# Modulation products on VectorE alone, the mixer's gate first, branch weights loaded a part ahead

## Chip, cores and metric

The kernel runs on one core of one Trainium2 chip. The metric is the device time of one execution in microseconds (us). The time before is the median of three runs.

## What is computed

Two layers of a diffusion backbone over 256 latent tokens and 256 context tokens of width 1024. Each layer first computes six modulation vectors per stream from a conditioning vector, then four token mixers in parallel, then a mixture of experts. Cut to what the change touches:

```python
s_lat = silu(c); s_ctx = silu(c_ctx)[None]
for l in range(2):
    mod_lat = split(s_lat @ ada_w[l] + ada_b[l], 6)      # and mod_ctx likewise
    u = modulate(rms_norm(h, norm_mix_g[l]), mod[0], mod[1])
    y = token_mixer(u, ...)                              # four branches, gated, then @ w_out
    h = h + mod[2] * y                                   # the mixer's gate
    u = modulate(rms_norm(h, norm_ffn_g[l]), mod[3], mod[4])
    h = h + mod[5] * expert_choice_ffn(u)                # 16 experts
```

In layer 1 only the latent stream goes on past the keys and values.

## The kernel before, in words

**Stages.** By the profile, layer 0's mixer runs to about 710 us, its experts to about 1165, layer 1's mixer to about 1560, its experts to the end. In a mixer, TensorE (PE) multiplies the normalized tokens by the input projection. Every fp32 factor is split into a high part (a cast on ScalarE, ACT, L348) and a low part (a subtraction on VectorE, DVE, L349), and three products are summed (L355 to L357). Beside this stream run the branches: `hyena`, `conformer` (31 taps a channel on DVE, L1246), `mla` (latent attention; its softmax rows are scaled at L1418) and `diff` (differential attention). `branch` multiplies each branch's output by its weights, which it loads (L1028) and splits itself.

**Modulation.** The first two of the six vectors of layer 0 are made by PE at the start (`modulation`). All others come from `products`, as weighted sums without PE. They are made in groups `(layer, g)`, where g = 0, 1, 2 stands for vectors 0 and 1, 2 and 3, or 4 and 5. A group has 2048 outputs, in 16 chunks of 128 rows; each chunk comes in two halves of 512 weights, so a group is 32 jobs. A job loads a 128x512 weight tile (`aw`, 256 KB), multiplies it by the activated conditioning row (`cb`) and sums along the row, once for each stream that is needed: twice in layer 0, once in layer 1. Layer 0 makes the groups (0,2), (0,1) and (1,0): 96 jobs, 192 products. Layer 1 makes (1,2) and (1,1): 64 jobs, 64 products.

A product is done in one of two ways. On DVE it is one fused `scalar_tensor_tensor` that also sums (L526; the profile shows a second short instruction that reads the accumulator). On GpSimd (POOL) it is a multiplication (L528), and ACT sums it afterwards with a copy (L507). `ND` says how many of a group's 16 chunks go to DVE: 6 in layer 0, none in layer 1. So layer 0 has 72 products on DVE and 120 on POOL, layer 1 has 64 on POOL. `half(True)` issues those of DVE, `half(False)` those of POOL and ACT. `end` puts the sums together and, for g = 1 and 2, makes rows of them (L577 on POOL, then PE and ACT). The output projection waits for g = 1 (L974), `router` for g = 1 and 2.

**Order.** Instructions are issued in an order found while the kernel is built. Every part is a generator. `Order.run` goes through the list of them and takes the first that is due at the planned time of PE; a generator yields a cost per engine, an event to wait for, or the time at which it is due again. Costs are in `_a`, `_d` and `_q`: 0.60 us for a 512-wide DVE instruction, and no cost for DVE and POOL holding each other up. `PACE` is added to the planned end of a job before the next is due. `MVP` gives the place of the products in the list: 1 in layer 0, directly behind the loader of the weight stream, and 5 in layer 1. `S.wait` delays two generators by 0.7 us; it names them by their number in the whole list (41 and 51: `rope("k")` and the `end` of group (1,2) of layer 1). Each engine then works through its own queue in that order, and so does the DMA queue of SP.

**Buffers.** Twelve tiles of 128x2048 (`big`) hold the weight stream and what it multiplies; forty of 128x512 (`t2`) hold the rest. In layer 0 the conditioning rows take one `big` tile until the products are done. The residual stream `h` has eight tiles of its own; five of them hold filter tables during layer 0's mixer, and `residual` loads the tokens into all eight after `hyena` (L1618).

Of the kernel before, what the change touches and what calls it, by code (L numbers as in the profile page):

```python
# [226 lines left out]
def kernel(ctx: ExitStack, tc: tile.TileContext, x, ctxt, cols, skip, lamb, fng, ta, tb, tcn, td,  # L227
# [7 lines left out]
    NB, NT2 = 12, 40  # L235
    ND, PACE, AHEAD = (6, 0), ((0.5, -2), (3.0, -2.0)), 2
    PRE, PREW = (1, 3), (1, 3)
# [159 lines left out]
    def layer(l):  # L397
# [68 lines left out]
        def products(groups, ss, after):  # L466


            cb, cb_ev = {}, Ev()
            ends = {g: [None, None, Ev()] for g in groups}  # L470
            nd = ND[l]

            def rows():

                yield after
                if not last:
                    yield from S.until(room())
                    row = big("cb")
                for s in ss:
                    for i in range(2):  # L480
                        cb[s, i] = t2("cb") if last else row[:, (2 * s + i) * 512:(2 * s + i + 1) * 512]
                        nc.sync.dma_start(cb[s, i], bass.AP(tensor=cc.tensor, offset=cc.offset + s * D + i * 512,
                                                            ap=[[0, 128], [1, 512]]))
# [9 lines left out]
            def half(dve):  # L493
                jobs = [(lm, g, c, k) for lm, g in groups for c in (range(nd) if dve else range(nd, 16)) for k in range(2)]
                held, w = [], {}
# [7 lines left out]
                def summed(till):  # L503
                    n = 0
                    while held and held[0][2] <= till:
                        o, a, _ = held.pop(0)
                        nc.scalar.activation(o, o, AF.Copy, accum_out=a)  # L507
                        n += 1
                    return {"act": n * _a(512)}

                if jobs:
                    yield cb_ev
                    for i in range(AHEAD):
                        load(i)
                for i, (lm, g, c, k) in enumerate(jobs):
                    load(i + AHEAD)
                    wt_, arr = w.pop(i)
                    yield arr
                    if ends[lm, g][dve] is None:
                        n = nd if dve else 16 - nd  # L520
                        ends[lm, g][dve] = sm(4 * n, "ad" if dve else "ap", bufs=3).rearrange("p (s c k) -> p s c k", s=2, k=2)
                    new = []
                    for s in ss:
                        o, a = wt_ if s == ss[-1] else t2("aj" if dve else "ao"), ends[lm, g][dve][:, s, c if dve else c - nd, k:k + 1]
                        if dve:
                            nc.vector.scalar_tensor_tensor(o, wt_, 1.0, cb[s, k], op0=OP.mult, op1=OP.mult, accum_out=a)  # L526
                        else:
                            nc.gpsimd.tensor_tensor(o, wt_, cb[s, k], op=OP.mult)  # L528
                            new.append((o, a))
                    del wt_, o  # L530
                    if dve:
                        e = yield {"dve": len(ss) * (_d(512) + 0.07)}
                        yield e + PACE[l][0]
                    else:
                        e = yield {"pool": len(ss) * _q(512)}
                        yield summed(S.t["pe"])
                        held.extend((o, a, e) for o, a in new)
                        del new
                        yield e + PACE[l][1]
                    if c == (nd - 1 if dve else 15) and k == 1:  # L540
                        e = yield summed(e)
                        ends[lm, g].append(e)
                        if len(ends[lm, g]) == 3 + (0 < nd) + (nd < 16):
                            ends[lm, g][2].t = max(ends[lm, g][3:]) + 1.0
                            if not last and (lm, g) == groups[-1]:
                                drop()

            def end(lm, g, r):
                m = mods[lm]
                yield ends[lm, g][2]  # L550
                dst = m["B" if g == 0 else f"c{g}"]
                n = r.stop - r.start
                for dve, c0, c1 in ((True, 0, nd), (False, nd, 16)):
                    if c1 > c0:
                        a, t = ends[lm, g][dve], sm(32, "as", bufs=1).rearrange("p (s c) -> p s c", s=2)[:, r, c0:c1]
                        nc.vector.tensor_tensor(t, a[:, r, :, 0], a[:, r, :, 1], op=OP.add)
                        nc.vector.scalar_tensor_tensor(dst[:, r, c0:c1], t, 0.5, col(lm, "ada_b")[:, None, g * 16 + c0:g * 16 + c1]
                                                       .to_broadcast([128, n, c1 - c0]), op0=OP.mult, op1=OP.add)
                if g != 1:
# [26 lines left out]

            return [end(lm, g, slice(ss[0], 2)) for lm, g in groups] + [rows(), half(True), half(False)]

# [271 lines left out]
        h_ev = {(t, n): Ev() for t in tchunks for n in range(4)}  # L860
        gates_done, br_ev = Ev(), Ev()

        def stream(items):
# [65 lines left out]
            def body():  # L929
# [43 lines left out]
                gates_done.t = S.t["pe"]  # L973
                yield mods[l]["ev"][1]  # L974
                for k in range(KC):
                    yield acc_ev[k]
# [37 lines left out]

        def branch(i, os, k0, ready):
            nk = len(os)
            yield ready
            if not accs:
                yield from S.until(room(ns))
                accs.extend(big("acc") for _ in range(ns))  # L1020
            ws, arr = {}, {}
# [19 lines left out]

            CUT = {"act": nk / 2 * _a(512), "dve": nk / 2 * _d(512)}
            for d2 in range(BA[l]):
                load(d2)
            yield tg_ev[i, 0]
            yield arr[0]
# [264 lines left out]
        kv_n, cq_n = {}, {}  # L1311
        ml_done = Ev()
        o_ml = [None] * 2
# [20 lines left out]
        def mla():  # L1334
# [69 lines left out]
            del wuq, wukv, cqT, kvT, krT  # L1404
            yield e
            scale = 96.0 ** -0.5
            for c in range(2):
# [206 lines left out]
        def residual():  # L1614
            yield hy_done
            for t in range(4):
                for n in range(2):
                    nc.sync.dma_start(h[t][n], tokens(t)[:, n * 512:(n + 1) * 512])  # L1618

        head, body = stream(items)  # L1620
# [8 lines left out]
        if l == 0:  # L1629
            gens += [lambdas(), residual()]  # L1630
        gens += [hyena(), mla(), rope("k"), rope("q"), diff(),
                 branch(1, o_hy, 4, hy_done), branch(2, o_cf, 6, cf_done), branch(3, o_ml, 8, ml_done),
                 branch(0, o_df, 0, df_done)]
        mv = products([(l, 2), (l, 1)] + ([] if last else [(l + 1, 0)]), (1,) if last else (0, 1), u_ev)
        mv_at = MVP[l]
# [9 lines left out]
        xe, top = {}, {}  # L1645
        rt_ev, x_ev = Ev(), [Ev(), Ev()]
        r_tok = [const.tile([128, 1], F32, name=f"rtok{l}{t}") for t in range(4)]
# [78 lines left out]
        def router():  # L1726
# [14 lines left out]
            nc.vector.tensor_copy(cb[:, :R], p[:, :R])  # L1741
            yield {"pe": 1.0, "dve": 0.1}

        def route(t):

            s, i = t // 2, streams.index(t // 2)
            s4, ss = sm(4, "ss4"), sm(1, "ss")
            b, e, hT = t % 2, 0.0, None

            def logits(n):  # L1750
# [402 lines left out]
```

## Time and profile before

| | |
|---|---|
| median of 3 runs | 2030.7 us (2025.22 to 2036.47) |
| the profiled execution | 2030.58 us, of which the span from first to last instruction is 2028.8 us |
| busy, share of the span | PE 84%, DVE 48%, ACT 28%, POOL 25% |
| mean granted clock of TensorE | 0.907 |
| moved by DMA | 550.75 MB, 271 GB/s over the span |

The shares are means over stages with different limits. The stages are told apart by the windows, which give the busy time of each engine in a stretch of the span.

### The profile page before, as it was taken

The page shows a single profiled execution, that of the slowest core. Times are in us where ns is not written, and L with a number is a line of the kernel's source. Part 1 is how long each engine was busy: PE and PEld are TensorE (multiplying, and loading weights), DVE is VectorE, ACT ScalarE, POOL GpSimd, SP SyncE. Part 2 cuts the span into 40 slices and gives each one's busy share as a digit, 9 for nine tenths or more (in the row PEclk, how much of TensorE's full clock was granted, in tenths as well). Part 3 has the DMA queues.
Part 4 walks back from the last instruction along what each step waited for, and adds up shares of the span by engine and source line. Part 5 has one row for each costly group of instructions (what it writes and reads, how often), then busy time and mean ns, then how long its engine had stood idle before and what let it go on. Part 6 is the DMA issues. An engine that isn't in the chain of part 4 may idle for free.

```text
span 2028.8 us, 28213 instructions
## 1 busy us (share of the span) xinstructions
PE 1713.3 (84%) x11128; PEld 1109.7 (55%) x11128; DVE 973.3 (48%) x1690; ACT 573.0 (28%) x1301; POOL 503.6 (25%) x413
## 2 busy tenths in 40 slices
PE   5889787899999899989999789988998867676665
PEld 2669465676788844334333268877997433322222
DVE  4787898977644412223332176778665111111012
ACT  4443454544432110001100063566552000000000
POOL 1565797803110100000010033777321000000000
PEclk8998888999999999989999999998998977777677
DMA  7534534331235599999999964555579999999997
GB/s 277 192 110 133 177 125 139 114 113 52 67 98 220 181 343 399 418 416 417 415 415 419 410 198 144 161 181 176 169 234 355 405 411 413 415 414 411 414 414 295
DMA packets 204589, 550.75 MB, mean 271 GB/s; under 512 B 14054, under 2 KB 94120, under 8 KB 173992
## 3 DMA queue, kind: packets, MB, share of 16 engines
q1 hardware_dynamic: 204456, 548.94, 71.7%
q8 instruction: 88, 1.44, 0.3%
q14 instruction: 45, 0.37, 0.0%
HBM read 547.83 MB, written 1.05 MB: 271 GB/s over the span
## 4 chain that ended last, share of the span: by engine, by line
PE 46%; DMA 28%; DVE 15%; ACT 4%; issue 3%; POOL 3%; SPq 0%; ACTq 0%; DVEq 0%; POOLq 0%
PE pm L1973 10%; DMA we<-in_w_eo_dram 10%; DMA we<-in_w_ei_dram 9%; PE pm L355 6%; PE pm L357 6%; PE pm L356 6%; PE psc L1998 4%; DMA h<-in_w_ei_dram 3%; DMA h<-in_w_eo_dram 3%; DVE wq L349 3%; PE psc L1862 2%; DVE aj L526 1%; DVE aw L526 1%; ACT wq L348 1%; POOL aw L528 1%
## 5 line engine op out<-in xcount | busy, mean ns | idle before, releaser
L1973 PE MATMUL pm<-we,xe 128*32 128x256 f32 (+1 forms) x2912 | 407.1, 543 | 97.9 <-DMA we<-in_w_ei_dram 96.0
L1973 PEld LDWEIGHTS pm<-we,xe 128*32 128x32 f32 (+1 forms) x2912 | 136.0, 136 | 345.2 <-issue 186.9
L355 PE MATMUL pm<-uh,wq 128*128 128x256 f32 (+1 forms) x832 | 293.6, 353 | 17.7 <-ACT tg L1001 8.2
L356 PE MATMUL pm<-ul,wq 128*128 128x256 f32 (+1 forms) x832 | 285.7, 343 | 2.5 <-DVE ul L785 1.5
L357 PE MATMUL pm<-uh,wq 128*128 128x256 f32 (+1 forms) x832 | 285.0, 342 | 0.0
L349 DVE TENSOR_TENSOR wq<-wi,wq 128x1024 fp32r<-128x1024 f32 x131 | 182.5, 1404 | 114.0 <-ACT wq L348 113.9
L1985 DVE SCALAR_TENSOR_TENSOR ea<-ea,pm 128x512 f32<-128x512 f32 (+1 forms) x32 | 17.7, 554 | 428.5 <-ACT ea L1984 428.5
L1998 PE MATMUL psc<-we,eaT 128*32 128x256 f32 (+1 forms) x1280 | 171.6, 510 | 35.0 <-DMA we<-in_w_eo_dram 33.5
L528 POOL TENSOR_TENSOR aw<-aw,cb 128x512 f32<-128x512 f32 x124 | 192.8, 1568 | 16.7 <-DMA aw<-in_ada_t_dram 8.1
L355 PEld LDWEIGHTS pm<-uh,wq 128*128 128x128 f32 x832 | 163.4, 196 | 41.4 <-ACT tg L1001 9.1
L356 PEld LDWEIGHTS pm<-ul,wq 128*128 128x128 f32 x832 | 163.1, 196 | 20.6 <-issue 3.7
L357 PEld LDWEIGHTS pm<-uh,wq 128*128 128x128 f32 x832 | 163.4, 196 | 16.8
L2010 DVE TENSOR_TENSOR ye<-psc,modr 32x512 f32<-32x512 f32 (+1 forms) x120 | 66.4, 554 | 201.8 <-PE psc L1998 200.5
L1984 ACT ACTIVATE ea<-pm 128x512 f32<-128x512 f32 (+1 forms) x32 | 15.7, 491 | 483.1 <-PE pm L1973 483.1
L348 ACT CAST wq<-wi 128x1024 fp32r<-128x1024 f32 x132 | 136.2, 1044 | 15.2 <-DMA wi<-in_w_in_dram 13.0
L1998 PEld LDWEIGHTS psc<-we,eaT 128*32 128x32 f32 (+1 forms) x1280 | 58.7, 129 | 143.8 <-issue 74.3
L1902 POOL TENSOR_TENSOR hg<-h,gr 128x512 f32<-128x512 f32 x2 | 2.6, 1286 | 462.0 <-DMA gr<-in_fng_dram 458.1
L1246 DVE SCALAR_TENSOR_TENSOR ca<-up,colt,ca 128x510 f32<-128x510 f32 (+29 forms) x120 | 113.4, 945 | 2.3
L528 POOL TENSOR_TENSOR ao<-aw,cb 128x512 f32<-128x512 f32 x60 | 97.7, 1628 | 22.5 <-DMA aw<-in_ada_t_dram 19.5
L2042 ACT COPY eaT<-pt 128x512 f32<-128x512 f32 (+1 forms) x32 | 15.3, 479 | 273.9 <-PE pt L2040 273.9
L1292 ACT ACTIVATE e<-psc,nm 128x512 f32<-128x512 f32 (+1 forms) x72 | 44.3, 616 | 146.5 <-DVE nm L1290 146.1
L660 POOL MEMSET hf<- 1x256 f32 x4 | 1.5, 378 | 325.8 <-ACT ab L656 325.8
(408 smaller groups left out, 3005.0 us busy)
## 6 DMA issues: line engine op xcount, KB each, us to landing
we<-in_w_ei_dram SPq DMA_DIRECT2D x233, 1024.0 KB, 14.0
we<-in_w_eo_dram SPq DMA_DIRECT2D x110, 1024.0 KB, 14.6
wi<-in_w_in_dram SPq DMA_DIRECT2D x58, 1024.0 KB, 5.4
aw<-in_ada_t_dram SPq DMA_DIRECT2D x160, 256.0 KB, 5.5
we<-in_w_ei_dram SPq DMA_DIRECT2D x52, 256.0 KB, 8.1
wbr<-in_w_branch_dram SPq DMA_DIRECT2D x40, 256.0 KB, 5.3
h<-in_w_ei_dram SPq DMA_DIRECT2D x40, 256.0 KB, 16.3
h<-in_w_eo_dram SPq DMA_DIRECT2D x40, 256.0 KB, 16.3
```

What stands on the lines that cost most here:

```text
L348: nc.scalar.copy(hi, src)
L349: eng.tensor_tensor(lo, src, hi.bitcast(F32), op=OP.subtract)
L355: nc.tensor.matmul(out, lh, rh, start=first and i == 0, stop=False)
L356: nc.tensor.matmul(out, lh, rl, start=False, stop=False)
L357: nc.tensor.matmul(out, ll, rh, start=False, stop=last and i == n - 1)
L526: nc.vector.scalar_tensor_tensor(o, wt_, 1.0, cb[s, k], op0=OP.mult, op1=OP.mult, accum_out=a)
L528: nc.gpsimd.tensor_tensor(o, wt_, cb[s, k], op=OP.mult)
L1246: nc.vector.scalar_tensor_tensor(o, up[:, :, max(d, 0):256 + min(d, 0)], cw[:, c0 + d:c0 + d + 1], o, op0=OP.mult, op1=OP.add)
L1292: nc.scalar.activation(e, p[:, :nk], AF.Exp, scale=scale, bias=nm, accum_out=s)
L1973: nc.tensor.matmul(dst[j * M:(j + 1) * M, :], lhs, w[o + j * FW // 512][:, j * FW % 512:j * FW % 512 + FW], start=k == 0, stop=k == KC - 1 ...
L1998: nc.tensor.matmul(py[j * M:(j + 1) * M, :FW], aT[:, c * 128 + q * M:c * 128 + (q + 1) * M], w[f % 2 * 2 + j * FW // 512][:, j * FW % 512: ...
L2010: nc.vector.tensor_tensor(ye[eg][s][c0 // 512][e4 * CAP:(e4 + 1) * CAP, c0 % 512:c0 % 512 + FW], py[r0:r0 + CAP, :FW], mod5[r0:r0 + CAP, c ...
```

## The change

All products are fused instructions on DVE; `half` is one generator. The order of groups is (l,1), (l,2), then (1,0) in layer 0. The pace is 0.0 in layer 0 and -1.5 in layer 1. In layer 1 the rows are loaded and the products begin once the latent tokens are normalized (`lat_ev`), before the context's are. In layer 0 the conditioning rows lie in three tiles of `h` and one `t2` tile; so `residual` loads five tiles after `hyena` and three after the last product, and the output projection waits for that in the plan. `branch` loads its first weights at an earlier event (`early`) than that of its input. `route` waits for `router` in the plan. With one generator less per layer, numbers 41 and 51 of the list are `rows` and `conformer` of layer 1.

```diff
-    ND, PACE, AHEAD = (6, 0), ((0.5, -2), (3.0, -2.0)), 2
+    PACE, AHEAD = (0.0, -1.5), 2
...
             def rows():
                 yield after
-                if not last:
-                    yield from S.until(room())
-                    row = big("cb")
                 for s in ss:
                     for i in range(2):
-                        cb[s, i] = t2("cb") if last else row[:, (2 * s + i) * 512:(2 * s + i + 1) * 512]
+                        cb[s, i] = t2("cb") if last or (s, i) == (0, 0) else h[s + 2][i]
...
-                        o, a = wt_ if s == ss[-1] else t2("aj" if dve else "ao"), ends[lm, g][dve][:, s, c if dve else c - nd, k:k + 1]
-                        if dve:
-                            nc.vector.scalar_tensor_tensor(o, wt_, 1.0, cb[s, k], op0=OP.mult, op1=OP.mult, accum_out=a)
-                        else:
-                            nc.gpsimd.tensor_tensor(o, wt_, cb[s, k], op=OP.mult)
-                            new.append((o, a))
+                        o = wt_ if s == ss[-1] else t2("aj")
+                        nc.vector.scalar_tensor_tensor(o, wt_, 1.0, cb[s, k], op0=OP.mult, op1=OP.mult,
+                                                       accum_out=ends[lm, g][0][:, s, c, k:k + 1])
                     del wt_, o
-                    if dve:
-                        e = yield {"dve": len(ss) * (_d(512) + 0.07)}
-                        yield e + PACE[l][0]
-                    else:
-                        e = yield {"pool": len(ss) * _q(512)}
-                        yield summed(S.t["pe"])
-                        held.extend((o, a, e) for o, a in new)
-                        del new
-                        yield e + PACE[l][1]
+                    e = yield {"dve": len(ss) * (_d(512) + 0.07)}
+                    yield e + PACE[l]
+                    if c == 15 and k == 1:
+                        ends[lm, g][1].t = e + 1.0
+                prod_ev.t = e
...
                 yield mods[l]["ev"][1]
+                if l == 0:
+                    yield res_ev
...
-        def branch(i, os, k0, ready):
+        def branch(i, os, k0, ready, early):
             nk = len(os)
-            yield ready
-            if not accs:
-                yield from S.until(room(ns))
-                accs.extend(big("acc") for _ in range(ns))
...
+            yield early
             for d2 in range(BA[l]):
                 load(d2)
+            yield ready
+            if not accs:
+                yield from S.until(room(ns))
+                accs.extend(big("acc") for _ in range(ns))
...
         def residual():
-            yield hy_done
-            for t in range(4):
-                for n in range(2):
+            for ev, part in ((hy_done, range(5)), (prod_ev, range(5, 8))):
+                yield ev
+                for i in part:
+                    t, n = i // 2, i % 2
                     nc.sync.dma_start(h[t][n], tokens(t)[:, n * 512:(n + 1) * 512])
+                yield S.load(0.25 * len(part))
+            res_ev.t = 0.0
...
-                 branch(1, o_hy, 4, hy_done), branch(2, o_cf, 6, cf_done), branch(3, o_ml, 8, ml_done),
-                 branch(0, o_df, 0, df_done)]
-        mv = products([(l, 2), (l, 1)] + ([] if last else [(l + 1, 0)]), (1,) if last else (0, 1), u_ev)
+                 branch(1, o_hy, 4, hy_done, k_ev), branch(2, o_cf, 6, cf_done, cfa_ev[1][0]),
+                 branch(3, o_ml, 8, ml_done, ml_mid), branch(0, o_df, 0, df_done, df_mid)]
+        mv = products([(l, 1), (l, 2)] + ([] if last else [(l + 1, 0)]), (1,) if last else (0, 1), lat_ev if last else u_ev)
...
-            yield {"pe": 1.0, "dve": 0.1}
+            rw_ev.t = yield {"pe": 1.0, "dve": 0.1}
         def route(t):
...
+            yield rw_ev
```

## Rows read from the trace of the kernel before

**Rows 1.** The page: busy us (share) x instructions; busy tenths in 40 slices of 50.7 us

```profile
PE 1713.3 (84%) x11128; PEld 1109.7 (55%) x11128; DVE 973.3 (48%) x1690; ACT 573.0 (28%) x1301; POOL 503.6 (25%) x413
...
DVE  4787898977644412223332176778665111111012
...
DMA  7534534331235599999999964555579999999997
```

**Rows 2.** Windows: length, busy of PE, PEld, DVE, ACT, POOL, then PEclk, DMA share, GB/s

```profile
50.00:400.00 350.00, 288.93 (x1310) 221.60 (x1311) 301.00 (x416) 165.07 (x406) 254.03 (x183) 0.90 0.43 142
400.00:620.00 220.00, 214.11 (x1114) 171.26 (x1114) 137.29 (x267) 95.37 (x199) 35.26 (x32) 1.00 0.27 82
...
720.00:1165.00 445.00, 416.21 (x1914) 157.29 (x1912) 113.01 (x201) 36.70 (x71) 6.93 (x9) 0.97 1.01 406
...
1200.00:1450.00 250.00, 222.34 (x1641) 200.10 (x1640) 194.82 (x306) 142.87 (x342) 154.96 (x125) 0.96 0.52 165
...
1560.00:2029.00 469.00, 319.23 (x3341) 138.04 (x3340) 72.20 (x178) 22.35 (x58) 3.68 (x4) 0.76 0.99 399
```

**Rows 3.** Waits of PE, 40 to 400 us: total us, times, longest

```profile
PE pt L1298 <- DVE e L1418: 16.1, 4, 8.1
PE psc L1369 <- DVE rp L1360: 9.6, 1, 9.6
...
PE psc L357 <- DVE wbrl L349: 4.5, 2, 2.9
```

**Rows 4.** The chain that ended last, 0 to 720 us: start, us, what

```profile
203.93 4.39 DVE wq L349 x2
208.32 1.69 DVE aj L526 x2
...
213.60 1.98 PE psc L1369 x2
```

**Rows 5.** Lines 526 and 528, 0 to 420 us: ns min/median/max, first and last start

```profile
L526 DVE SCALAR_TENSOR_TENSOR aj<-aw,cb x36: 624/1632/1809, 86.1 to 391.3; 128x512 f32<-128x512 f32 x36
...
L526 DVE DVE_READ_ACCUMULATOR aj<-aw,cb x36: 73/77/84, 87.8 to 393.0; 128x1 f32 x36
L526 DVE SCALAR_TENSOR_TENSOR aw<-aw,cb x36: 691/1631/1819, 87.9 to 393.1; 128x512 f32<-128x512 f32 x36
...
L528 POOL TENSOR_TENSOR ao<-aw,cb x60: 1255/1712/2291, 89.0 to 399.0; 128x512 f32<-128x512 f32 x60
```

**Rows 6.** Windows of lines 526 (DVE), 528 (POOL, both stretches) and 507 (ACT, both) alone

```profile
50.00:400.00 350.00, 95.92 (x144) 0.90 0.43 142
...
50.00:400.00 350.00, 191.56 (x119) 0.90 0.43 142
1200.00:1450.00 250.00, 95.61 (x64) 0.96 0.52 165
...
50.00:400.00 350.00, 77.27 (x235) 0.90 0.43 142
1200.00:1450.00 250.00, 42.84 (x128) 0.96 0.52 165
```

**Rows 7.** Lines of DVE, 50 to 400 us: busy us, mean ns; idle before, releaser

```profile
L1246 DVE SCALAR_TENSOR_TENSOR ca<-up,colt,ca 128x510 f32<-128x510 f32 (+14 forms) x43 | 52.5, 1221 | 0.8
L349 DVE TENSOR_TENSOR wq<-wi,wq 128x1024 fp32r<-128x1024 f32 x33 | 52.3, 1596 | 22.4 <-ACT wq L348 22.4
```

**Rows 8.** The same view, 420 to 700 us, where no products run

```profile
L349 DVE TENSOR_TENSOR wq<-wi,wq 128x1024 fp32r<-128x1024 f32 x30 | 37.7, 1263 | 47.1 <-ACT wq L348 47.1
...
L1246 DVE SCALAR_TENSOR_TENSOR ca<-up,colt,ca 128x490 f32<-128x490 f32 (+4 forms) x10 | 7.2, 722 | 0.2
```

**Rows 9.** Waits of PE, 1165 to 1560 us

```profile
PE pm L355 <- ACT tg L1001: 8.2, 4, 6.2
```

**Rows 10.** The chain that ended last, 1130 to 1560 us

```profile
1383.50 6.96 POOL aw L528 x5
```

**Rows 11.** Tile wbr, its DMA issues on SP: ns min/median/max, first and last start

```profile
L1028 SPq DMA_DIRECT2D wbr<-in_w_branch_dram x40: 368/379/1633, 201.0 to 1513.5; - x40
```

More of the change, by code (lines that the diff above doesn't have):

```diff
@@ L469, in products @@
             cb, cb_ev = {}, Ev()
-            ends = {g: [None, None, Ev()] for g in groups}
-            nd = ND[l]
+            ends = {g: [None, Ev()] for g in groups}
             def rows():
                 yield after
-                if not last:
-                    yield from S.until(room())
-                    row = big("cb")
                 for s in ss:
                     for i in range(2):
-                        cb[s, i] = t2("cb") if last else row[:, (2 * s + i) * 512:(2 * s + i + 1) * 512]
+                        cb[s, i] = t2("cb") if last or (s, i) == (0, 0) else h[s + 2][i]
                         nc.sync.dma_start(cb[s, i], bass.AP(tensor=cc.tensor, offset=cc.offset + s * D + i * 512,
@@ L491, in rows, with half @@
                 cb_ev.t = S.t["dve"]
-            def half(dve):
-                jobs = [(lm, g, c, k) for lm, g in groups for c in (range(nd) if dve else range(nd, 16)) for k in range(2)]
-                held, w = [], {}
+            def half():
+                jobs = [(lm, g, c, k) for lm, g in groups for c in range(16) for k in range(2)]
+                w = {}
                 def load(i):
@@ L501, in load @@
                         w[i] = load2(ada_t[lm, r:r + 128, k * 512:(k + 1) * 512], "aw"), S.load(0.25)
[L503 to L514, printed above, removed]
+                yield cb_ev
+                for i in range(AHEAD):
+                    load(i)
                 for i, (lm, g, c, k) in enumerate(jobs):
@@ L518, in half @@
                     yield arr
[L519 to L522, printed above, removed]
+                    if ends[lm, g][0] is None:
+                        ends[lm, g][0] = sm(64, "ad", bufs=3).rearrange("p (s c k) -> p s c k", s=2, k=2)
                     for s in ss:
-                        o, a = wt_ if s == ss[-1] else t2("aj" if dve else "ao"), ends[lm, g][dve][:, s, c if dve else c - nd, k:k + 1]
-                        if dve:
-                            nc.vector.scalar_tensor_tensor(o, wt_, 1.0, cb[s, k], op0=OP.mult, op1=OP.mult, accum_out=a)
-                        else:
-                            nc.gpsimd.tensor_tensor(o, wt_, cb[s, k], op=OP.mult)
-                            new.append((o, a))
@@ L530, in half @@
-                    del wt_, o
-                    if dve:
-                        e = yield {"dve": len(ss) * (_d(512) + 0.07)}
-                        yield e + PACE[l][0]
-                    else:
-                        e = yield {"pool": len(ss) * _q(512)}
-                        yield summed(S.t["pe"])
-                        held.extend((o, a, e) for o, a in new)
-                        del new
-                        yield e + PACE[l][1]
[L540 to L546, printed above, removed]
+                        o = wt_ if s == ss[-1] else t2("aj")
@@ L549, in end @@
                 m = mods[lm]
-                yield ends[lm, g][2]
+                yield ends[lm, g][1]
                 dst = m["B" if g == 0 else f"c{g}"]
                 n = r.stop - r.start
[L553 to L558, printed above, removed]
+                a, t = ends[lm, g][0], sm(32, "as", bufs=1).rearrange("p (s c) -> p s c", s=2)[:, r]
@@ L559, in end @@
+                nc.vector.tensor_tensor(t, a[:, r, :, 0], a[:, r, :, 1], op=OP.add)
+                nc.vector.scalar_tensor_tensor(dst[:, r], t, 0.5, col(lm, "ada_b")[:, None, g * 16:g * 16 + 16]
+                                               .to_broadcast([128, n, 16]), op0=OP.mult, op1=OP.add)
                 if g != 1:
@@ L585, in end @@
                 m["ev"][g].t = e
-            return [end(lm, g, slice(ss[0], 2)) for lm, g in groups] + [rows(), half(True), half(False)]
+            return [end(lm, g, slice(ss[0], 2)) for lm, g in groups] + [rows(), half()]
         def filters(lf, after=None):
@@ L860, in layer @@
         h_ev = {(t, n): Ev() for t in tchunks for n in range(4)}
-        gates_done, br_ev = Ev(), Ev()
+        gates_done, br_ev, prod_ev, res_ev = Ev(), Ev(), Ev(), Ev()
         def stream(items):
@@ L1311, in layer @@
         kv_n, cq_n = {}, {}
-        ml_done = Ev()
+        ml_done, ml_mid = Ev(), Ev()
         o_ml = [None] * 2
@@ L1405, in mla @@
             yield e
+            ml_mid.t = e
             scale = 96.0 ** -0.5
@@ L1645, in layer @@
         xe, top = {}, {}
-        rt_ev, x_ev = Ev(), [Ev(), Ev()]
+        rt_ev, rw_ev, x_ev = Ev(), Ev(), [Ev(), Ev()]
         r_tok = [const.tile([128, 1], F32, name=f"rtok{l}{t}") for t in range(4)]
```

## The prediction

> **What bounds the kernel now.** I read the page first: its engine line and slices [rows 1]. No engine is the bound everywhere. DMA reads 9 tenths only in two stretches, and DVE is high only in two others. The windows by stage [rows 2] put numbers on that. The experts of layer 0 (720 to 1165) and of layer 1 (1560 to 2029) run at a DMA share of 1.01 and 0.99: they last as long as their weights take to arrive, and the change leaves their bytes alone. They only start earlier or later, with the end of the mixer before them. The products, as the kernel calls the weighted sums, lie in two stretches: 50 to 400 us in layer 0 and 1200 to 1450 in layer 1. The forecast is made there.
>
> In 50 to 400 PE is busy 288.9 of 350 us, so it stands idle for 61 us, and its mean granted clock is 0.90. The clock knows 2.4 and 1.2 GHz; 10% below full over 350 us is worth 35 us. From 400 to 620 PE is busy 214 of 220 at clock 1.00: there nothing is to be had [rows 2]. So in layer 0 at most some 61 us of idle time and a part of the 35 us can come back.
>
> Who makes PE wait in 50 to 400? The list of waits names DVE: 16.1 us for the scaled attention rows of L1418, 9.6 us for one rope step [rows 3]. The chain of that place shows how such a wait is made: two weight splits take 4.39 us and a product 1.69 us, both ahead of the rope step for which PE waits until 213.6 [rows 4]. Both are stretched. A fused product takes 0.62 to 0.69 us at its shortest and 1.63 at the median; a POOL product takes 1.26 at its shortest and 1.71 at the median [rows 5]. The same split takes 1.60 us in this stretch and 1.26 in 420 to 700, where no products run; a convolution tap takes 1.22 against 0.72 [rows 7, 8]. So DVE and POOL hold each other up, and a third of the products on DVE already costs 95.9 us [rows 6].
>
> **Part 1, layer 0: 120 products go from POOL to DVE.** POOL loses 191.6 of its 254.0 us and ACT loses 77.3 of accumulation [rows 2, 6]. DVE work, at quiet prices:
> - products: 192 x (0.69 + 0.08 us for reading the accumulator) = 148 [rows 5], in place of 96 for 72;
> - all else: 301.0 - 95.9 = 205; less 43 taps x 0.50 = 21.5 and 33 splits x 0.33 = 11 [rows 7, 8], so 172.6.
>
> That makes 320 us against 301 now. DVE gets no lighter: what 120 products add (92) is somewhat more than what the contention gives back (46 on its own products, 32 on taps and splits). To it comes the contention with the other 62.5 us of POOL work: nothing at least; at most every us of it, 62.5. The rows show 78 us lost for 254 us of POOL work, 0.31 each, so 19; some of that is still within the 172.6, since I took the stretch off taps and splits alone. I take 10, near that row: 330.
>
> Trainium skill, "SBUF — State Buffer", Who interferes with whom: the shared port pair is an exclusive lock, held for a whole instruction, and a DVE instruction with two SBUF inputs contends with a POOL instruction that reads SBUF. By that rule alone a pair would take 0.69 + 1.26 = 1.95 us and all 62.5 us of the other POOL work would count, so that the sum of DVE would be 382. The trace agrees on who contends, but its pairs go by in about 1.7. By the lock alone the stretch would be 382 + 15 - 25 = 372 us, 22 more than now, on the side of the slower rival below.
>
> DVE's idle time is 49 us now, 22.4 of it waits for ACT's half of a split [rows 2, 7]. ACT gets 77 us back and a product fills any gap, so I leave 15 (from 0 to 49). Not all products need lie in this stretch: DVE has 220 - 137 = 83 us idle from 400 to 620 [rows 2]. The last of the three groups, 64 products or 49 us, serves layer 1 alone. The planner gives a product its turn when DVE's planned queue has run down (place 1 in the list, pace 0), so only some slip over; I take 25 us (from 0 to 49). Length of the stretch: 330 + 15 - 25 = 320, **30 us less**. Ends: 320 + 0 - 49 = 271, but PE's own work is 289 - 35 = 254 and never ran gapless, so 290, 60 less; above, 330 + 49 - 0 = 379, 29 more.
>
> Why should PE go along? Its waits are for DVE results behind a queue, and each block in that queue gets shorter: a pair of products 1.54 us instead of 3.3, a split 1.26 instead of 1.60. And the planner costs a pair at 1.35 us: the order written by it is near to what the chip does when nothing stretches.
>
> **Part 2, layer 1: 64 products, all on POOL now, go to DVE.** POOL loses 95.6 us of 155, ACT 42.8 [rows 2, 6]. Here the products stand in the way on those two: PE waits 8.2 us for ACT's gate tanh [rows 9], and 7 us of the chain are POOL products in a row [rows 10], with the normalization of the differential heads behind them in POOL's order. DVE is busy 194.8 of 250; with 49 more that is 244 if contention gives nothing back, or 205 if it gives back the fifth that it takes from DVE's other work in layer 0 (32.5 of 205, and some on smaller operations). The products may start once the latent rows are normalized, so before 1200, which spreads them further. PE's idle time is 27.7 us and its clock 0.96 is worth 10 [rows 2]. I take **10 us less**; ends 25 less (most of the idle time) and 15 more (a third of the 49 us on the path).
>
> **The small parts.** Branch weights a part ahead: no wait on their DMA is in the list; the 4.5 us of PE are for their split on DVE [rows 3], counted above. The 40 issues of 0.38 us [rows 11] on SP only move; ahead of a wi load they cost it that much and the ring's weights lie ready. I take 0, up to 5 more if the held buffers delay others. Residual loads in two parts: 3 of 8 issues move behind the products, hidden by the 220 us of gates and branches before the output projection; if the plan's end of the products is too early, SP stands in that wait with the wi loads behind it: 0 to 10 more. The freed `big` buffer, the mixer's gate first, and the router's wait: 0, since PE has only 6 us of idle time in 400 to 620, where the modulation would be waited for. The planner's two 0.7 us delays now fall on other workers (the rows and the conformer of layer 1): 0, either sign, a few us.
>
> **Sum.** The profiled execution took 2030.58 us, as the median of 2030.7. 2030.6 - 30 - 10 = **1990 us**. Added ends: 2030.6 - 60 - 25 = 1945 and 2030.6 + 29 + 15 + 5 + 10 = 2090.
>
> **Rivals.**
> - *VectorE becomes the bound (slower).* Place: 50 to 400, where DVE wants 330 us at least if all products come early, as place 1 in the list makes them. If DVE keeps its present share of the stretch, 301 of 350 (0.86), it needs 330 / 0.86 = 384, 34 more; with layer 1 level, **2065**. It decides from the point where DVE is busy over 95% of the stretch and PE's waits on it pass the 61 us of idle. For it: 0.86 already, and 120 products more on the fullest engine. Against: the gaps in DVE's row are waits that products can fill. Trainium skill, "Perfetto Trace Analysis", Optimizing Scalar/DVE Operations: when DVE is saturated, moving work to ScalarE or GpSimd may make sense, though between DVE and GpSimd it might not help. The first half speaks against this change, the second for its being a wash; the trace has both, 0.86 busy and pairs at 1.7. Chance 0.2.
> - *A wash.* Shorter blocks, but 2.7 times as many, and PE waits as long as before: 350 + 0 to 10 less in layer 0, 0 in layer 1: **2025**. Speaks for it that DVE's sum hardly changes. Chance 0.18.
> - *Nearly all waits go.* PE runs the stretch as it runs 400 to 620: 60 less, and 25 less in layer 1: **1945**. Against it: DVE must shed 49 us past 400. Chance 0.1.
> - *It doesn't do what it says*: SP stuck behind the late residual loads, or the branch loads crowding out others. It would be seen as DMA waits before splits; 10 us, within the wash.
>
> **How the numbers follow.** Forecast 0.52 (1965 to 2015 by itself), all waits 0.1, wash 0.18, slower 0.2. A measurement of this kernel tells about 0.5%, 10 us, from no change. Faster than 2020.5: 0.52 + 0.1 + 0.03 of the wash = 0.65. Within: 0.16, the rest of the wash and a little of the slower case. Slower than 2041: 0.19. The range goes from 1955 to 2048: it leaves out half of the case below and some 0.14 above.
>
> **What would show it.** Right: products at about 0.7 us and splits at 1.25 throughout; DVE over 90% busy up to some 370 us; PE idle under 40 us in 50 to 400 with the clock above 0.93; no POOL product and no accumulation on ACT; the experts' stages as long as before, only earlier. Wrong: DVE at 97% with PE idle above 60 us (the slower rival), products still at 1.2 us or more (the remaining POOL work costs what the lock says), or a gain that is lost again between 400 and 720.

## The result and the profile after

The changed kernel takes 2001.56 us (median of 4 runs, 1998.93 to 2005.31) against 2029.6 for the kernel before in the same comparison: a ratio of 0.9874, 95% interval 0.9853 to 0.9894, 28 us less. The forecast was 1990, 40 less.

The page of the changed kernel: busy times, and slices of 50.0 us.

```profile
PE 1700.4 (85%) x11128; PEld 1108.5 (55%) x11128; DVE 971.6 (49%) x2052; ACT 461.8 (23%) x933; POOL 217.3 (11%) x229
...
PE   5998999887999899899899788998988867666665
...
DVE  4886789877764312212432285888864111111012
...
PEclk8999999888999899989999998999998877787777
DMA  7443334423345799999999954565759999999997
```

Against [rows 1], POOL lost 286 us and ACT 111, and DVE's total stayed where it was: the products that came added about as much busy time as the shorter instructions gave back. The windows by stage, with the columns of [rows 2]:

```profile
50.00:370.00 320.00, 305.08 (x1585) 244.81 (x1582) 259.32 (x540) 112.52 (x213) 58.89 (x56) 0.98 0.41 134
370.00:600.00 230.00, 190.84 (x856) 148.36 (x855) 172.91 (x380) 75.94 (x154) 39.08 (x38) 0.90 0.34 108
...
696.00:1140.00 444.00, 416.45 (x1916) 157.63 (x1914) 112.95 (x201) 36.70 (x71) 6.92 (x9) 0.97 1.01 408
1175.00:1425.00 250.00, 232.98 (x1725) 212.18 (x1725) 198.76 (x429) 110.67 (x225) 63.11 (x64) 0.96 0.56 179
...
1535.00:2002.00 467.00, 316.81 (x3340) 137.94 (x3340) 67.04 (x160) 22.36 (x58) 3.66 (x4) 0.77 0.99 397
```

Layer 0 is told by two windows. From 50 to 370 us PE has done 1585 matmuls; before, it had done 1310 from 50 to 400. It idles 15 us of 320, with the clock at 0.98. Then it turns: from 370 to 600 PE stands idle for 39 us with the clock at 0.90, where the kernel before, from 400 to 620, had 6 us at 1.00. By 600 it has done 2441; before, 2424 by 620. The kernel before reaches 1585 matmuls at 441 us:

```profile
50.00:441.00 391.00, 329.93 (x1585) 255.99 (x1586) 332.68 (x484) 186.34 (x457) 256.12 (x184) 0.91 0.41 137
```

So, counted in matmuls done, a lead of 71 us at 370 has shrunk to some 20 at 600. The experts' stages keep their length (444 and 467 us) and DMA share, and only start earlier.

The instructions themselves became what the forecast said. The products' own line, one half of those of layer 0 (ns min/median/max, first and last start):

```profile
L510 DVE SCALAR_TENSOR_TENSOR aw<-aw,h x96: 691/692/1660, 82.3 to 583.7; 128x512 f32<-128x512 f32 x96
L510 DVE DVE_READ_ACCUMULATOR aw<-aw,h x96: 76/81/85, 83.8 to 584.3; 128x1 f32 x96
```

The median fell from 1.63 us [rows 5] to 0.69. But the last product starts at 584 us, not at 399. The windows of this line alone show how the products spread:

```profile
50.00:370.00 320.00, 84.55 (x224) 0.98 0.41 134
370.00:600.00 230.00, 63.60 (x160) 0.90 0.34 108
```

What PE waits for from 370 to 600 (total us, times, longest):

```profile
PE psc L355 <- ACT wbrh L348: 21.9, 3, 12.4
PE psc L355 <- ACT e L1264: 5.7, 3, 3.3
PE pt L1230 <- DVE ol L1510: 4.0, 1, 4.0
```

In the kernel before, all of PE's waits listed for 40 to 400 add up to 49.0 us that end with DVE, 11.3 with ACT and 5.8 with POOL. In the changed kernel, 40 to 370, they are 12.8 with DVE, 7.1 with ACT and none with POOL. Of the two longest of [rows 3] the first is gone, and of the other this is left:

```profile
PE psc L1341 <- DVE rp L1332: 2.3, 1, 2.3
```

Behind 370, PE waits mostly for casts of branch weights on ACT, and ACT in that stretch waits for DVE:

```profile
ACT e L1264 <- DVE nm L1262: 53.4, 18, 6.6
```

### The profile page after: what moved, and what is told of

Read it like the earlier page. It is cut to its first block, busy times and chain, and to the rows that moved or that the text cites. A ratio compares the mean times of both kernels' runs of the same rounds, so it can differ in the third digit from the quotient of the medians.

```text
span 2001.9 us, 27922 instructions
## 1 busy us (share of the span) xinstructions
PE 1700.4 (85%) x11128; PEld 1108.5 (55%) x11128; DVE 971.6 (49%) x2052; ACT 461.8 (23%) x933; POOL 217.3 (11%) x229
## 4 chain that ended last, share of the span: by engine, by line
PE 48%; DMA 26%; DVE 14%; issue 6%; ACT 5%; POOL 1%; SPq 0%; ACTq 0%; DVEq 0%; POOLq 0%
DMA we<-in_w_ei_dram 14%; PE pm L1951 10%; DMA we<-in_w_eo_dram 7%; PE pm L355 7%; PE pm L357 6%; PE pm L356 6%; PE psc L1976 4%; DVE wq L349 3%; DMA h<-in_w_eo_dram 3%; PE psc L1840 2%; DVE aw L510 2%; PE psc L355 2%; ACT wq L348 1%; PE psc L357 1%; PE psc L356 1%
## 5 line engine op out<-in xcount | busy, mean ns | idle before, releaser
L349 DVE TENSOR_TENSOR wq<-wi,wq 128x1024 fp32r<-128x1024 f32 x131 | 164.1, 1263 | 91.9 <-ACT wq L348 91.5
L1218 DVE SCALAR_TENSOR_TENSOR ca<-up,colt,ca 128x510 f32<-128x510 f32 (+29 forms) x120 | 80.8, 673 | 2.1
L355 PE MATMUL pm<-wq,uh 128*128 128x256 f32 (+1 forms) x240 | 72.7, 303 | 8.1 <-DVE rsq L319 4.0
L510 DVE SCALAR_TENSOR_TENSOR aw<-aw,h 128x512 f32<-128x512 f32 x96 | 77.1, 803 | 3.6
L356 PE MATMUL pm<-wq,uh 128*128 128x256 f32 (+1 forms) x240 | 70.7, 295 | 0.0
L357 PE MATMUL pm<-wq,ul 128*128 128x256 f32 (+1 forms) x240 | 70.7, 295 | 0.0
```

The source lines that it names most:

```text
L349: eng.tensor_tensor(lo, src, hi.bitcast(F32), op=OP.subtract)
L355: nc.tensor.matmul(out, lh, rh, start=first and i == 0, stop=False)
L356: nc.tensor.matmul(out, lh, rl, start=False, stop=False)
L357: nc.tensor.matmul(out, ll, rh, start=False, stop=last and i == n - 1)
L1218: nc.vector.scalar_tensor_tensor(o, up[:, :, max(d, 0):256 + min(d, 0)], cw[:, c0 + d:c0 + d + 1], o, op0=OP.mult, op1=OP.add)
```

## The experiments

All times are medians in us, with the ratio to the kernel before of the same comparison. Where stages are compared, this table holds; its marks are read from one profiled execution of each kernel, so a few us between two rows mean little: the first gated product of the output projection in layer 0, the first matmul with the output weights of layer 0's last expert, the first gated product in layer 1, and the time from the second to the third.

```
run                        layer 0   last expert   layer 1   length
before                       646.3        1164.5    1531.9    367.4
changed                      622.4        1139.4    1502.1    362.7
products alone               638.5        1154.6    1511.5    356.9
branch loads late            625.5        1142.9    1516.6    373.7
POOL reads back              693.4        1211.2    1623.1    411.9
short products               590.7        1107.4    1454.7    347.3
short POOL products          580.0        1097.2    1436.7    339.5
pace early                   616.6        1133.5    1497.2    363.7
rows in big                  622.9        1139.8    1504.7    364.9
order back                   609.1        1127.1    1492.7    365.6
branch loads early alone     644.2        1162.5    1532.9    370.4
order back, loads late       622.5        1138.4    1512.6    374.2
order back, pace early       624.4        1140.9    1508.5    367.6
order back, measured costs   635.4        1154.0    1518.5    364.5
```

**1. Products alone**, in the kernel before:

```diff
-    ND, PACE, AHEAD = (6, 0), ((0.5, -2), (3.0, -2.0)), 2
+    ND, PACE, AHEAD = (16, 16), ((0.0, -2), (-1.5, -2.0)), 2
```

> The kernel before with nothing changed but where the products run: all 16 chunks on DVE in both layers, pace 0.0 and -1.5. Branch loads, order of groups, buffers and residual loads stay as before. If the gain comes from taking the products off POOL and ACT: 2000 to 2010 us, a ratio to before of 0.985 to 0.990, products at 0.7 us and splits at 1.25 us. If it comes from the other parts of the change (branch weights ahead, the freed buffer, the order of groups): 2020 to 2035 us.

Measured: 2017.88 (2011.89 to 2018.73), ratio 0.9952 (0.9932 to 0.9973). Between the two: some four tenths of the gain. The profiled run is the fastest of its runs, 6 us under the median, so its row in the table flatters it. There layer 1 gains 10.5 us, as the forecast had it, and layer 0 only 8.

**2. Branch loads late**, in the changed kernel:

```diff
-branch(1, o_hy, 4, hy_done, k_ev), branch(2, o_cf, 6, cf_done, cfa_ev[1][0])
-branch(3, o_ml, 8, ml_done, ml_mid), branch(0, o_df, 0, df_done, df_mid)
+branch(1, o_hy, 4, hy_done, hy_done), branch(2, o_cf, 6, cf_done, cf_done)
+branch(3, o_ml, 8, ml_done, ml_done), branch(0, o_df, 0, df_done, df_done)
```

> The changed kernel with the branch weights loaded when the branch's input is ready, as before. If that part is worth nothing, as forecast: within 5 us of the changed kernel, 1997 to 2007 us. If it carries a part of the gain: 2010 us or more, with PE waiting for casts of branch weights that stand behind a DMA.

Measured: 2019.47 (2015.16 to 2026.29), ratio 0.9966 (0.995 to 0.9983), 0.9% or 18 us above the changed kernel. A part that I had put at nothing carries more than the products do alone. The table puts 3 us of it into layer 0 and 11 into layer 1. SP's queue of this run at that place (start, us, what, how many) and the chain there show the 11:

```profile
1487.13 9.79 SPq L1678 DMA_DIRECT2D we<-in_w_ei_dram  x5
1497.02 1.88 SPq L1676 DMA_DIRECT2D we<-in_w_ei_dram  x4
1498.99 0.44 SPq L995 DMA_DIRECT2D wbr<-in_w_branch_dram  x1
```

```profile
1497.94 0.12 PE psc L355
1498.99 10.32 DMA wbr<-in_w_branch_dram
1509.39 0.63 ACT wbrh L348
1510.06 0.58 PE psc L355
```

The last part of the branch weights, 256 KB, is issued behind nine loads of expert weights, 6 MB together, that SP has just sent off. It lands 10.3 us later, where the median of these loads in this run is 5.1. ACT, DVE and PE all stand. Loaded a part ahead, it goes out before the experts'.

**3. POOL reads back**, in the changed kernel:

```diff
-                        o = wt_ if s == ss[-1] else t2("aj")
+                        o = t2("aj")
+                        for q in range(3 if last or c >= 6 else 0):
+                            nc.gpsimd.tensor_tensor(scr, wt_[:, q * 160:q * 160 + 192], cb[s, k][:, q * 160:q * 160 + 192], op=OP.mult)
```

> The changed kernel with three POOL multiplications of 192 columns of the same weight tile added beside as many products as POOL had before (120 and 64); their result goes to a scratch tile that nobody reads, the plan doesn't count them, the output stays the same. If contention between POOL and DVE is the mechanism: products and splits get back to 1.2 us and more, and the time goes to 2035 us or above, beyond the kernel before, since DVE now carries all products. If the engine that does the products matters only through POOL's and ACT's queues or through the order: 2000 to 2015 us.

Measured: 2124.09 (one run), 122 above the changed kernel, in both mixers (71 us by the output projection of layer 0, 49 in the length of layer 1). DVE's lines in 50 to 400 (busy us, mean ns):

```profile
L513 DVE SCALAR_TENSOR_TENSOR aj<-aw,h 128x512 f32<-128x512 f32 x84 | 78.3, 956 | 0.5 <-POOL scr L512 0.5
L349 DVE TENSOR_TENSOR wq<-wi,wq 128x1024 fp32r<-128x1024 f32 x39 | 53.5, 1383 | 21.8 <-ACT wq L348 21.8
```

DVE's instructions stretch (means of 0.96 and 1.38 against 0.74 and 1.22 in the changed kernel up to 370), less than I expected, and the time goes further up than I expected. What this run can't tell apart: the added work also stands in POOL's queue in front of work for which the mixers wait, and the products' results take a tile more.

**4. Short products**, in the changed kernel:

```diff
-nc.vector.scalar_tensor_tensor(o, wt_, 1.0, cb[s, k], ...
+nc.vector.scalar_tensor_tensor(o[:, :32], wt_[:, :32], 1.0, cb[s, k][:, :32], ...
```

> The changed kernel with each product over 32 of 512 columns, so that the sums leave out the rest; the order, the loads and the waits stay. DVE loses some 130 us of work in layer 0 and 30 in layer 1. If the products still hold PE up (PE idle between 370 and 600 us, where DVE is shared by products, attention rows and branch splits): 1965 to 1985 us. If DVE no longer matters: 1995 to 2003 us.

Measured: 1956.34 (1952.94 to 1959.94), ratio 0.9662 (0.9639 to 0.9685): 43 us below the changed kernel by the ratios, more than expected, though DVE's products lost only 95 us in layer 0 (148 to 53), not 130. The products' time on DVE is still on the path. PE's window and its longest wait (the window 370 to 580 here, 370 to 600 for the wait):

```profile
370.00:580.00 210.00, 189.68 (x887) 150.05 (x888) 133.55 (x367) 77.60 (x154) 34.91 (x38) 0.95 0.37 122
```

```profile
PE psc L355 <- ACT wbrh L348: 18.3, 3, 10.3
```

PE idles 20 us there, against 39 in the changed kernel. But its waits for casts of branch weights hardly shrink (18.3 against 21.9 us), so most of them do not come from the length of the products. The same waits are 20.4 us in run 1 and about 1 in the kernel before and in run 5: they are there where the plan puts all products on DVE.

**5. Short POOL products**, in the kernel before:

```diff
-nc.gpsimd.tensor_tensor(o, wt_, cb[s, k], op=OP.mult)
+nc.gpsimd.tensor_tensor(o[:, :32], wt_[:, :32], cb[s, k][:, :32], op=OP.mult)
...
-nc.scalar.activation(o, o, AF.Copy, accum_out=a)
+nc.scalar.activation(o[:, :32], o[:, :32], AF.Copy, accum_out=a)
```

> The kernel before with each POOL product and its sum on ACT over 32 of 512 columns, so that those sums leave out the rest; order, loads and waits stay, and 72 products stay on DVE at full width. It shows what POOL's products and ACT's sums cost before the change, without more work on DVE. If contention and those two queues hold the mixers up: splits at 1.25 us, 1955 to 1980 us in all. If DVE's own work is the bound and POOL's part was hidden: 2010 to 2028 us.

Measured: 1933.16 (1930.98 to 1936.11), ratio 0.9539 (0.9499 to 0.958), 92 us less. So POOL's products and their sums at full width cost 92 us while they ran beside everything else. The lines of DVE in 50 to 400 and the windows:

```profile
L349 DVE TENSOR_TENSOR wq<-wi,wq 128x1024 fp32r<-128x1024 f32 x41 | 50.6, 1245 | 52.3 <-ACT wq L348 52.3
...
L526 DVE SCALAR_TENSOR_TENSOR aw<-aw,cb 128x512 f32<-128x512 f32 x36 | 27.3, 757 | 1.2
```

```profile
50.00:370.00 320.00, 302.69 (x1568) 240.02 (x1567) 241.08 (x478) 140.08 (x455) 120.22 (x185) 0.97 0.48 163
370.00:580.00 210.00, 203.91 (x995) 162.81 (x995) 122.75 (x227) 83.25 (x162) 33.17 (x30) 1.00 0.30 100
```

With POOL's reads cut short the split takes 1.25 and the product 0.76, and PE goes as fast to 370 as in the changed kernel. PE's waits in 40 to 400 that end with DVE fall from 49.0 to 10.8 us, those with ACT stay (11.3 and 11.6), those with POOL fall from 5.8 to 0.9: what comes back reaches PE through DVE. How much of the 92 us is the stretch of DVE's instructions and how much the queues of POOL and ACT further back, no run separates. In the 210 us from 370 to 580 DVE has only 123 us of work, against 159 in the changed kernel:

```profile
370.00:580.00 210.00, 170.84 (x766) 131.81 (x765) 158.75 (x353) 68.66 (x142) 38.46 (x37) 0.89 0.35 111
```

PE idles 6 us there, against 39. This is the gain of the change without its price, since 120 products are cut short here and none is moved.

**6. Pace early**, in the changed kernel: `PACE` of layer 0 from 0.0 to -1.5.

> The changed kernel with the pace of layer 0's products at -1.5 in place of 0.0, so that they are planned earlier and closer together. If the products' late end (584 us, in the stretch of the differential attention) is what eats a part of the gain: they end before 500 us and the output projection starts earlier than at 622 us, 1985 to 1997 us. If VectorE becomes the bound as soon as products crowd in front of hyena and mla: the output projection starts later and the time is 2008 to 2025 us.

Measured: 1996.75 (1995.5 to 2000.11), ratio 0.986 (0.9819 to 0.99). The products end at 495 us and the output projection starts 6 us earlier; the intervals of the two ratios overlap. It is not slower, so crowding the products is no harm by itself; that their late end was the price is not shown: 43 us of products are left after 370 in place of 64, and PE still idles 32 us between 370 and 600.

**7. Rows in big**, in the changed kernel: the conditioning rows of layer 0 in a `big` tile (as in the lines taken out above), `drop()` after the last group, and

```diff
-            for ev, part in ((hy_done, range(5)), (prod_ev, range(5, 8))):
+            for ev, part in ((hy_done, range(8)),):
```

> The changed kernel with layer 0's conditioning rows in one of the twelve big tiles again, and all residual loads after hyena, as before. Products alone brought the output projection of layer 0 8 us forward, the whole change 24; late branch loads cost 3 of it. If the freed big tile is the rest: the output projection of layer 0 starts at 632 to 640 us and the time is 2010 to 2018 us. If it is not (order of groups, numbers in the list): within 4 us of the changed kernel.

Measured: 2002.91 (1998.13 to 2006.41), ratio 0.9878 (0.9836 to 0.9919). The freed tile is worth nothing that these times show.

**8. Order back**, in the changed kernel: `products([(l, 2), (l, 1)] + ...`.

> The changed kernel with the groups in the order (l,2), (l,1) again. Nothing waits for the gate before the output projection, which comes after the last product: if so, within 4 us of the changed kernel, 1997 to 2006 us. If the order is what the rest of the gain in layer 0 hangs on: 2010 us or more.

Measured: 1990.14 (1989.67 to 1992.96), ratio 0.9822 (0.9782 to 0.9861): a miss on the good side. It ran on the same chip as run 7, whose fastest run is above its slowest. So "the mixer's gate first" costs some 11 us by the ratios, whose intervals just overlap (13 against run 7); in the profiled executions all of it lies in layer 0. PE's windows are the same up to 370; the difference lies behind it:

```profile
50.00:370.00 320.00, 305.01 (x1588) 244.83 (x1587) 259.77 (x541) 112.80 (x214) 61.17 (x64) 0.98 0.40 134
370.00:600.00 230.00, 201.14 (x912) 156.65 (x911) 179.43 (x386) 78.98 (x158) 37.40 (x30) 0.93 0.35 117
```

912 matmuls in place of 856, and 11.6 us of waits for casts of branch weights in place of 21.9. Of all kernels that compute everything, this one was the fastest.

**9. Branch loads early alone**, in the kernel before: the new `branch` with its four events, and nothing else.

> The kernel before with nothing changed but the branch weights, loaded at the earlier events; the products stay on POOL and DVE. In the trace of before no cast of branch weights waited for a DMA. If early loads pay only once the mixer runs faster (as the late ones cost 18 us in the changed kernel): within 6 us of before, 2019 to 2031 us. If they are worth 18 us by themselves: 2003 to 2012 us.

Measured: 2037.5 (2027.88 to 2042.86), ratio 1.0045 (1.0021 to 1.007). A miss: no gain by itself but a loss of some 9 us, with the interval clear of 1. Where it is lost no run shows; by the table it is in neither mixer to more than 3 us.

**10. Order back, loads late**, in the changed kernel: runs 2 and 8 together.

> The changed kernel with both undone: groups in the order (l,2), (l,1) and branch weights loaded late. With early loads the old order gave 1990 us. If the two parts add up: 2004 to 2012 us. If they are tied to each other, by the plan that comes out of both: 1990 to 2000 or 2015 to 2025 us. Products alone gave 2018 us; where this is near, the freed buffer, the earlier start in layer 1 and the numbers in the list are worth nothing.

Measured: 2017.03 (2012.29 to 2018.47), ratio 0.9934 (0.991 to 0.9959). By the ratios the old order gives 0.3% with late loads (against run 2) and 0.5% with early ones (run 8 against the changed kernel), and the intervals overlap in both. If the parts simply added up, the ratio would be 0.991, which is just inside the interval. That they are tied is so only in the profiled executions, where the old order brings the output projection of layer 0 forward by 3 us with late loads and by 13 with early ones; the times do not show it. This kernel is also where the products alone stand (run 1, 0.9952): what sets the two apart, the freed tile, the residual loads in two parts, the earlier start in layer 1, the router's wait and the numbers in the list, is together worth nothing that these times show. Layer 1 shows the wait of run 2 again, 11.1 us:

```profile
1493.82 11.10 DMA wbr<-in_w_branch_dram
```

**11. Order back, pace early**, in the changed kernel: runs 6 and 8 together.

> The changed kernel with the old order of groups and the pace of layer 0 at -1.5. Alone they gave 1990 and 1997 us against 2002. If they add up: 1982 to 1988 us. If both only remove the same wait in the stretch of the differential attention: 1988 to 1997 us.

Measured: 2008.3 (2001.87 to 2009.16), ratio 0.9885 (0.986 to 0.9911). On top of run 8 the early pace costs some 13 us by the ratios, whose intervals overlap a little; on its own (run 6) it made no difference clear of noise. I have no cause for this that a run shows.

**12. Order back, measured costs**, in the changed kernel, beside the order:

```diff
 def _d(n):
-    return 0.07 + n / 960
+    return 0.15 + n / 960
...
-                    e = yield {"dve": len(ss) * (_d(512) + 0.07)}
+                    e = yield {"dve": len(ss) * (_d(512) + 0.08)}
```

> The changed kernel with the old order of groups and the plan's costs of DVE set to what the quiet trace shows (0.15 us + n/960, and 0.08 us for reading an accumulator, in place of 0.07 and 0.07). If PE's waits that are left come from a plan that takes DVE for faster than it is: 1972 to 1986 us. If they come from DVE's load whatever the plan says: 1986 to 1998 us.

Measured: 2023.3 (2018.47 to 2025.35), ratio 0.9967 (0.9952 to 0.9982): a miss, 29 us above run 8 by the ratios. Most of it is one wait. The plan now ends the products later; SP's queue (start, us, what), PE's waits at 600 to 650 and the chain there:

```profile
605.30 2.53 SPq L1678 DMA_DIRECT2D we<-in_w_ei_dram  x5
607.94 3.10 SPq L1676 DMA_DIRECT2D we<-in_w_ei_dram  x4
613.36 12.84 SPq L283 DMA_DIRECT2D aw<-in_ada_t_dram  x7
633.95 1.28 SPq L1593 DMA_DIRECT2D h<-in_x_dram  x3
```

```profile
PE pt L1742 <- POOL h L961: 23.1, 1, 23.1
```

```profile
613.36 11.76 DMA aw<-in_ada_t_dram
625.14 0.71 DVE aj L510 x2
...
633.96 0.71 DVE aw L510 x2
635.94 0.73 POOL h L961
```

The last product weights stand behind nine expert loads, and the first of them lands 11.8 us after its issue; DVE stands for 12.2 us, then does the last products one behind the other until 634.6. Only then comes the output projection's first gated product, at 635.4, and PE waits for the sum that follows it. So the wait is the products' own, late and ahead of the output projection in DVE's queue. The three last residual loads go out at 633.95, and nothing in this chain waits for them.

## Why the prediction was right, and where it was not

**Direction, stage and mechanism: right.** The gain lies in the two mixers, the experts' stages only shift, and DVE's sum hardly moved (973 to 972 us). The shape that was to show it is there: products at 0.69 us, splits at 1.22 to 1.26, PE idle under 40 us and a clock above 0.93 up to 400. One sign failed: DVE is busy 259 of 320 us up to 370, 81% and not over 90. The Trainium skill, "SBUF — State Buffer", Who interferes with whom, says that a DVE instruction with two SBUF inputs contends with a POOL instruction that reads SBUF; the trace agrees: with those reads cut to 32 columns (run 5) the splits of the kernel before take 1.25 us instead of 1.60. That the shared pair is held for a whole instruction the page says of DVE's 2-port modes; the forecast took it for these instructions too, and their 1.63 and 1.71 us beside each other [rows 5] are not the 1.95 that it worked out from that.

**Part 1 (30 less): 24 by the mark of the output projection, in part by luck.** Products cost 148 us on DVE, as computed. But the 1310 matmuls that the kernel before has done by 400 are done here by 328:

```profile
50.00:328.00 278.00, 263.74 (x1314) 210.36 (x1311) 224.51 (x455) 94.17 (x172) 58.89 (x56) 0.98 0.42 136
```

So the stretch got 72 us shorter, more than the 60 that the forecast had as its end, and some 48 of these were lost again behind it, where the forecast had no loss at all. The 24 come near the 30 because two errors offset each other. By 328 only 73 of the 148 us of products are done: 75 slipped over, where the forecast took 25, and DVE idles 53 us, where it took 15. DVE's sum did not set the length of this stretch. (A slip in the working: the 46 us given back on DVE's own products leave out reading the accumulators; with them it is 41. The sum of 320 does not use it, and the 19 us of other contention would be 18. A tap fell to 0.80, not 0.72: the rows compared mix shapes.) The step that failed is "there nothing is to be had", which was read as "there nothing is to be lost". From 370 on what is left hangs on differential attention, whose first scores come 72 us earlier than before and whose last ones only 16:

```profile
L1547 PE MATMUL psc<-qk x64: 376/589/792, 325.9 to 533.8; 64*128 64x256 f32 x32, 64*128 64x512 f32 x32
```

In the kernel before this was 397.9 to 549.9. This is the forecast's own third sign of error, a gain lost again between 400 and 720, and it came in part. The runs show two things behind it. One is DVE's load: with the products cut short in the same order (run 4), PE idles 20 us from 370 to 580 in place of 39. The other seems to be the order that the plan finds: with much the same work on DVE there (123 us against 134 in run 4) but the order of the kernel before (run 5), it idles 6. Fewer products behind 370 changed little (run 6).

**Part 2 (10 less): 5 by the length of layer 1.** With the products alone it was 10.5. Each is one execution, and run 9, which leaves the products where they were, is 3 us off the kernel before in the other direction. So the direction holds and the size is not settled.

**The branch loads (0): wrong.** Late, they cost 18 us (run 2). The step said that no wait on their DMA is in the list, which was true of the kernel before; in a mixer that runs faster the same load falls behind the experts' loads. Run 9 shows that the part gains nothing where the mixer is slow; there it costs some 9 us. A step that hides now has to be asked again at the pace that the other steps make.

**The order of groups (0): wrong by some 11 us** (run 8). Whether that is tied to the early loads the times do not show (run 10). Nothing waits for the modulation, as said; the order changes which tiles and queue places the plan gives to others, and the stretch after 370 is sensitive to that. Which of its waits turned on it is not settled: no run took one of them alone.

**The residual loads (0 to 10 more):** no run shows a price. The 23 us of run 12 stand behind the product weights and the products, not behind these loads.

**The sum in one line.** POOL's products cost 92 us (run 5). Done on DVE they give that back and take most of it again: 82 us with the products alone (run 1 gains 0.48%, 10 us), 64 with the rest of the change around them. The slower rival had the place wrong (DVE was never the bound up to 370) but the price right in kind: the products' time on DVE is still on the path, 43 us of it (run 4).

## What to carry to other kernels

When work moves from an engine that disturbs a second one onto that second one, price both: what the disturbance costs (cut the work short where it is and time it) and what the work costs where it goes (cut it short there). A stretch without waits is not a stretch where added work is free; ask which engine's slack keeps it so. Where the order is found by a planner, test the work's length and the order apart: a run with the work cut short keeps the order. And a prefetch that is worth nothing in the old trace has to be priced at the new pace: look for large loads that the same queue sends off just ahead of it.

## What was not expected of the hardware

- POOL's multiplications and ACT's sums cost 92 us in this kernel (run 5) though neither engine was busy for more than 28% of the span; in 50 to 400 POOL was busy 254 of 350 us [rows 2].
- A 256 KB load right behind nine loads, 6 MB together, on the same queue took 10.3 us to land, twice the median of its kind in that run.
- A fused multiply and sum over 128x512 fp32 took 0.69 us, plus 0.08 for reading its accumulator, on a quiet DVE; POOL's multiplication took 1.26 at the shortest [rows 5] and ACT's sum some 0.65 (77.3 us for 119 of them [rows 6]), so the fused instruction replaced 1.9 us of engine time.
